# Blocks 2 and 3 of the last half of a down projection as two by two products, and the order of the last scaling

## The chip, the cores and the metric

The kernel runs on one core of one Trainium2 chip. A core has a matrix engine (TensorE, PE in the profile), a vector engine (VectorE, DVE), a scalar engine (ScalarE, ACT), GpSimd (POOL) and a queue engine (SyncE, SP); each works through its own list of instructions in order, and semaphores hold an instruction back until its inputs are there. The metric is the device time of one execution in microseconds (us); less is better. Weights stream in from HBM by DMA, matmuls read SBUF and write PSUM, which has eight banks of 512 float32 columns.

## What is computed

One layer of a streaming encoder on 512 positions of width 1024. The part that matters here is its end, the channel mixer and the final norm:

```python
    h = rms_norm(x, norm_ffn_g[l])
    up = causal_dwconv(h @ w_up[l], conv_ffn_w[l])
    a, b = jnp.split(up, 2, axis=-1)
    x = x + (jax.nn.silu(a) * b) @ w_down[l]
return rms_norm(x, norm_f_g)
```

`w_up` is 1024 x 5632, `w_down` 2816 x 1024. In front of this stand a norm, an input projection, a gated convolution and an attention branch, and their merge.

## The kernel before

All activations are kept transposed: 128 channels on the partitions and 512 positions along the free axis, as two halves of 256. Every product is made in a split precision: an operand is cut into a high part (rounded to the matmul's format, ScalarE, L245 for weights) and a low part (the rest, VectorE, L249), and a product is three matmuls of 128 x 128 by 128 x 256: high by high, low by high, high by low. The cut of a chunk of weights is called its split.

The 22 blocks of 128 hidden channels are made in two phases (`PHASES`): 12 blocks, then the part of the down projection that uses them, then 10 blocks and the rest of the down projection. The output has eight blocks `m` of 128 channels; `x1[:, m, :]` holds the running sum.

**Two by two steps.** For a pair of output blocks `i` (blocks 2i and 2i+1) and a pair of depth blocks `q` (2q and 2q+1), the four block products over both halves of the positions are made with seven products instead of eight. The seven use forms of the right operand: the blocks b11, b12, b21, b22 themselves and t1 to t4, differences of them. They lie in `gh` (high parts) and `gl` (low parts) at the pair's place with an offset: 0 is b11, 1 and 2 are b21 and b22, 3 and 4 are t1 and t2, 5 and 6 are t3 and t4, 7 is b12. `PROD` (L305) lists for each product the weight form, the offset, the bank and the half. A step takes two (i, q), and two chunks of weights: P with 6 x 128 columns (18 matmuls) and F with 8 x 128 columns (24 matmuls). F consists of sums of weight blocks that DMAs have made in DRAM long before: `group` lists three copies on SP's queue (L132) and three accumulating DMAs on POOL's queue (L135) for every two steps, and `tick` issues the next of them at certain chunks (L150). A chunk's matmuls with high weights come first, those with low weights last (`passes`, L284).

After the last step of an `i`, `combine` puts its four banks together into the two blocks: one ScalarE copy (L1029) and seven VectorE operations (L1030 to L1048). In the last phase `final_square` follows for each block: ScalarE squares it (L1060 or L1063), VectorE adds that to `ssq3` (L1064) and ScalarE multiplies the block by the norm's weights (L1065).

In the last phase, pairs i = 2 and i = 0 (blocks 4, 5, 0, 1) are done in five steps of two, numbered here 12 to 16, so P12, F12, ... F16. Blocks 2, 3, 6 and 7 are done as plain products over the last ten depth blocks (`PLAIN`), whose weights come in six chunks dp0 to dp5 cut at `PCUTS`. Blocks 2 and 3 come first, each with one matmul group, one add (L1154) and a final square. Blocks 6 and 7 come last and by halves of the positions: both blocks' first half (`pdA`), then the second half (`pdB`), and in between and behind it the sum of squares over the partitions by matmuls with ones (`pc_n`, L337), the reciprocal root (L342, L344), its spread over the partitions (`pb_n`, L351) and the scaling and the stores (`fin_out`, L1183).

**What sets the order.** TensorE's instructions run in the order written. On ScalarE and VectorE a scheduler orders the rest at build time: it follows the kernel's work in a model of its own and gives an engine, when it is free, the ready instruction that stands first in the program. Two rules are laid over that. A chunk's split goes into one of two buffers in turn, so it must wait for the matmuls of the chunk two before it: the high part for those with high weights, the low part for those with low weights. And small work (combinations, squares, the forms of a pair) is put on a list `later` with a cost in us; each split takes from the list what fits its budget (L205, budgets at L255: 1.6 us for a P chunk, 0.75 for F, 3.5 for a dp chunk), and what it takes is issued behind that split on its engine. `flush` empties the list up to what a step needs: the forms of a pair before its first use, or the readers of a bank before it is used anew.

The forms of the last pair, q = 10, are put on the list for the splits of P13 to P15: t1 and t3 at F13, t2 and t4 and the split of b11 and b12 at P14, then (L1002 for high, L1003 for low parts) b21 and b22 at F14, t3 with t4 and t1 with t2 at P15. Five buffers hold raw weights on their way from HBM (`load`, L202).

Of the kernel before, what the change touches and what calls it, by code (L numbers as in the profile page):

```python
# [10 lines left out]
AF = mybir.ActivationFunctionType  # L11
ALU = mybir.AluOpType

P = 128
# [32 lines left out]
STEPS = (  # L47
    tuple(((i, q), (i, q + 1)) for i, q in ((0, 0), (0, 2), (1, 0), (1, 2), (0, 4), (1, 4)))
    + tuple(((i, q), (i, q + 1)) for i in (3, 2) for q in (0, 2, 4)),
    (((2, 6), (2, 7)), ((2, 8), (2, 9)), ((0, 6), (0, 7)), ((0, 8), (2, 10)), ((0, 9), (0, 10))),  # L50
)
HELD = 2
GS = 3
NFF = len(STEPS[0]) + len(STEPS[1])

PLAIN = [(m, k) for m in (2, 3, 6, 7) for k in range(*PHASES[1])]
PCUTS = (0, 8, 16, 20, 28, 32, 40)


@with_exitstack  # L60
def block_kernel(ctx, tc, xT, vecs, wv, win, wmix, wo, wup, wst, wdp, outT):
# [54 lines left out]
    sums = {}  # L116
    groups = [[NFF + 2 * j, NFF + 2 * j + 1] for j in range(KB - GS)]
    ngate = len(groups)
    groups += [list(range(n, min(n + 2, NFF))) for n in range(0, NFF, 2)]
    todo = []  # L120

    def group(i):

        ns = groups[i]
        t = dsp.tile([P, len(ns), D], F32, tag=f"sum{i}", name=f"sum{i}")
        for k, n in enumerate(ns):
            sums[n] = t[:, k, :]
        w = wst[ns[0] : ns[-1] + 1].rearrange("n p c -> p n c")
        w, f = ((lambda a, b, z=z: z[:, :, a * P : b * P]) for z in (w, t))

        def copy(dst, src):
            return lambda: keep(nc.sync.dma_start(dst, src))  # L132

        def add(dst, src):
            return lambda: keep(nc.gpsimd.dma_start(dst, src, accum_op=ALU.add))  # L135

        return [
            copy(f(0, 4), w(6, 10)),
            add(f(0, 4), w(0, 4)),
            copy(f(4, 6), f(0, 2)),  # L140
            add(f(4, 6), w(2, 4)),
            copy(f(6, 8), f(4, 6)),
            add(f(6, 8), w(4, 6)),
        ]
# [7 lines left out]
            todo.pop(0)()  # L152

    def double(n):
        return [(f"P{n}", wst[n, :, : 6 * P], 6 * P), (f"F{n}", sums[n], D)]

    def gate_n(j):
        return [NFF + 2 * (j - GS) + d for d in range(2)]
# [147 lines left out]
        (1, 0, 2, 0), (2, 1, 0, 0), (6, 2, 0, 1), (0, 6, 1, 0), (3, 3, 1, 1), (5, 4, 2, 1), (4, 5, 3, 0),  # L306
    )

    def place_of(f, s_):
        c = 2 * (f % 3 if f < 6 else 3) + s_  # L310
        return slice(c * P, (c + 1) * P)

    def pair(ns, form, banks):
# [756 lines left out]

    def down(ph, n0):

        sets = ({0: X, 1: Y, 3: X, 2: Y}, {0: X, 2: Y})[ph]
        todo, wants = [], {}
        for n, d in enumerate(STEPS[ph]):
            for kind in "PF":
                prods = []
                for s_, (i, q) in enumerate(d):
                    for f, g, b, h in PROD:
                        if (f < 3) == (kind == "P"):  # L1080
                            wants.setdefault(f"{kind}{n0 + n}", []).append(("q", q))
                            prods.append((place_of(f, s_), i, place(ph, q) + g, b, h))
                todo.append((f"{kind}{n0 + n}", prods))
        users = [{(i, b) for _, i, _, b, _ in prods} for _, prods in todo]
        for n, (name, prods) in enumerate(todo):
            wh, wl = chunk(name)
            flush(wants[name])
            before = set().union(*users[:n])
            after = set().union(*users[n + 1 :])
            out = []  # L1090
            for cs, i, g, b, h in prods:
                if i not in open_:
                    flush(sets[i])
                    open_[i] = [bank(x, f"dn{ph}{i}{x}") for x in sets[i]]
                out.append((
                    open_[i][b][:, th[h]], (i, b), wh[:, cs], wl[:, cs], gh[:, g, :], gl[:, g, :],
                    (i, b) not in before and (ph, i) != (1, HELD), (i, b) not in after and (ph, i) != (0, HELD),
                ))
            passes(out, len(out))
            if name[0] == "F":  # L1100
                for i in sorted({i for _, i, *_ in prods}):
                    if (i, 0) not in after and (ph, i) != (0, HELD):
                        combine(ph, i, open_.pop(i), sets[i])
            split_next()
# [40 lines left out]
            mm3(p, wh, wl, gh[:, g, :], gl[:, g, :], opens and k == kall[0], closes and k == kall[-1])  # L1145

    plain.c = 0
    for m, b in ((2, 4), (3, 2)):
        flush((b,))
        p = bank(b, f"pd{m}")  # L1150
        for k in kall:
            for t in range(2):
                plain(m, t, (k,), p[:, th[t]], t == 0, t == 1)
        nc.vector.tensor_add(x1[:, m, :], p, x1[:, m, :])  # L1154
        later.append((0, 0.8, (), lambda m=m: final_square(m)))

    m6 = KB - 2
    fetch(3)
    wx = fp.tile([P, 6, 2 * P], F32R, tag="gr", name="wx").rearrange("p a b -> p (a b)")
    fetch(4, [wx[:, a : a + 4 * P] for a in (80, 752)])  # L1160
    fetch(5)
    flush()
    pdA, pdB6, pdB7 = bank(3, "pdA"), bank(5, "pdB6"), bank(0, "pdB7")
    pd = ((pdA[:, th[0]], pdA[:, th[1]]), (pdB6[:, th[0]], pdB7[:, th[0]]))

    def plain7(m, t, ks):
# [11 lines left out]
    def fin_col(t, sqs):  # L1178
        s_ = ssq3[:, halves[t]]
        nc.vector.tensor_add(s_, s_, sqs[0])  # L1180
        return rstd_col([s_, sqs[1]], 2, 6 + t, f"n3{t}")

    def fin_out(t, rc):  # L1183
        hs = halves[t]
        pb = rstd_bc(rc, 2, (1, 4)[t], f"n3{t}")[:, : S // 2]
        rs = fp.tile([P, S], F32, tag="fu", name=f"rs{t}", bufs=3)[:, : S // 2]
        nc.scalar.activation(rs, pb, AF.Copy)
        for g, (a, b) in enumerate(((0, 1), (1, 3), (6, 8), (3, 5), (5, 6))):
            y = x1[:, a:b, hs]
            eng, r = (nc.gpsimd, rs) if g == 2 else (nc.vector, pb)  # L1190
            eng.tensor_mul(y, y, r.unsqueeze(1).to_broadcast([P, b - a, S // 2]))
            keep((nc.sync, nc.scalar)[g % 2].dma_start(outT[:, a:b, hs], y))

    def warm_on(n):
# [1 line left out]
        for i in range(n):  # L1196
            keep(nc.tensor.matmul(warm_to, gh[:, i, :P], gl[:, i, :], start=True, stop=True))

    warm_to = bank(2, "warm_to")[:, : 2 * P]
    for m in range(2):  # L1200
        plain7(m, 0, kall)
    sqA = [fin_sum(0, 0), fin_sum(0, 1)]
# [17 lines left out]
def _layout(i):  # L1220

    import numpy as np

    i = {k: np.asarray(v) for k, v in i.items()}
    f = np.float32

    def cols(v):
        return v.reshape(-1, P).T

    def taps(w):  # L1230
        return w.reshape(3, -1, P).transpose(2, 1, 0)
# [24 lines left out]
    wvv = wi[:, 3 * CW + 2 * S : 3 * CW + 3 * S]  # L1256
    o = 3 * CW + 3 * S
    wf = wi[:, o : o + H]
    win = np.concatenate([blocks(wi[:, : 3 * CW]), blocks(wqk), blocks(wi[:, o + H :])])
    wv = np.concatenate([wvv[:, : 4 * HD], wf, wvv[:, 4 * HD :]], axis=1).reshape(KB, P, S + H)  # L1260
    wmix = np.concatenate([i["w_out_conv"][0], i["w_out_attn"][0]], axis=0)
    wup = blocks(i["w_up"][0])
    wup = np.stack([wup[:NP], wup[NP:]], axis=1).reshape(2 * NP, P, D)
    wdn = blocks(i["w_down"][0]).reshape(KB, P, NP, P)
    order = ((1, 1), (0, 0), (0, 1), (1, 0), (1, 0))
    wst = []
    for d in STEPS[0] + STEPS[1]:
        wst.append(np.concatenate([wdn[2 * i + m, :, 2 * q + k] for m, k in order for i, q in d], axis=1))
    for j in range(GS, KB):
        for d in range(2):  # L1270
            w = [
                win[20 + 8 * m + j][:, (2 * q + k) * P : (2 * q + k + 1) * P]
                for m, k in order for q in (2 * d, 2 * d + 1)
            ]
            wst.append(np.concatenate(w, axis=1))
    wst = np.stack(wst)
    wdp = np.concatenate([wdn[m, :, k] for m, k in PLAIN], axis=1)
    return {
        "xT": x.T.reshape(KB, P, S).transpose(1, 0, 2),
        "vecs": vecs,  # L1280
        "wv": wv,
        "win": win,
        "wmix": blocks(wmix),
        "wo": blocks(i["w_o"][0]),
        "wup": wup,
        "wst": wst,
        "wdp": wdp,
    }
# [24 lines left out]
```

## Time and profile before

| | us |
|---|---|
| median of 3 runs | 705.13 (704.12 to 705.4) |
| the profiled execution | 707.72 |
| its span, first to last instruction | 706.0 |
| steps of the last phase | 643.27 to 667.07 |
| blocks 2 and 3, plain | 667.07 to 680.67 |
| blocks 6 and 7, plain, first half | 680.67 to 687.47 |
| rest: second half, norm, scaling, stores | 687.47 to 706.0 |

Positions are counted from the start of the span. An entry of a timeline gives the start, the time (of a merged entry, from its first start to its last end), the engine, the line, the operation, its output and inputs, and in brackets the idle time before it and what ended it. A VectorE or ScalarE operation's time includes the end of its pipeline, so that the next can start a little before it is over. The granted clock of TensorE is 0.993 of full over the span.

### The profile page before, as it was taken

The page shows a single profiled execution, that of the slowest core. Times are in us where ns is not written, and L with a number is a line of the kernel's source. Part 1 is how long each engine was busy: PE and PEld are TensorE (multiplying, and loading weights), DVE is VectorE, ACT ScalarE, POOL GpSimd, SP SyncE. Part 2 cuts the span into 40 slices and gives each one's busy share as a digit, 9 for nine tenths or more (in the row PEclk, how much of TensorE's full clock was granted, in tenths as well). Part 3 has the DMA queues.
Part 4 walks back from the last instruction along what each step waited for, and adds up shares of the span by engine and source line. Part 5 has one row for each costly group of instructions (what it writes and reads, how often), then busy time and mean ns, then how long its engine had stood idle before and what let it go on. Part 6 is the DMA issues. An engine that isn't in the chain of part 4 may idle for free.

```text
span 706.0 us, 14566 instructions
## 1 busy us (share of the span) xinstructions
PE 694.1 (98%) x6017; PEld 692.2 (98%) x6017; DVE 494.1 (70%) x790; ACT 340.2 (48%) x538; POOL 155.8 (22%) x177
## 2 busy tenths in 40 slices
PE   9999999999989999999999999999999999999995
PEld 9999999999989999999999999999999999999995
DVE  6677777765586777764368777777774677877853
ACT  6664655544474444444354444545443344544642
POOL 4125645435221010224412122120000111100002
PEclk9999999999999999999999999999999999999998
DMA  8534776847864696866566675537765233224503
GB/s 280 167 130 99 178 205 149 197 86 214 208 179 128 180 243 212 278 208 186 103 156 166 193 144 167 143 83 231 206 201 155 90 100 111 84 83 130 177 1 120
DMA packets 49682, 112.42 MB, mean 159 GB/s; under 512 B 4656, under 2 KB 21168, under 8 KB 49616
## 3 DMA queue, kind: packets, MB, share of 16 engines
q1 hardware_dynamic: 35776, 91.89, 40.4%
q0 software_dynamic: 12576, 18.39, 16.2%
q10 hardware_dynamic: 1264, 1.22, 0.5%
q8 instruction: 47, 0.77, 0.5%
q14 instruction: 19, 0.16, 0.1%
HBM read 109.31 MB, written 30.41 MB: 198 GB/s over the span
## 4 chain that ended last, share of the span: by engine, by line
PE 92%; DMA 3%; DVE 1%; ACT 1%; issue 1%; POOL 1%; DVEq 0%; POOLq 0%; ACTq 0%
PE p_up L278 26%; PE dn L296 11%; PE p_in L278 10%; PE p_up L296 8%; PE gs L296 7%; PE p_wo L278 6%; PE yc L296 3%; PE ya L278 3%; PE p_g L278 3%; PE pd L278 2%; PE pa L457 2%; DMA sum<-in_wst_dram 2%; PE pb L459 2%; PE p_q L278 2%; PE p_k L278 2%; PE o L638 1%
## 5 line engine op out<-in xcount | busy, mean ns | idle before, releaser
L278 PE MATMUL p_up<-x1h,wh_up 128*128 128x256 f32 x536 | 104.6, 276 | 0.0
L278 PE MATMUL p_up<-x1h,wl_up 128*128 128x256 f32 x536 | 104.4, 276 | 0.0
L278 PE MATMUL p_up<-x1l,wh_up 128*128 128x256 f32 x536 | 104.3, 276 | 0.0
L245 ACT ACTIVATE wh_up<-raw_up 128x1024 fp32r<-128x1024 f32 x44 | 46.7, 1060 | 89.1 <-PE p_up L278 68.8
L278 PEld LDWEIGHTS p_up<-x1h,wh_up 128*128 128x128 f32 x536 | 80.8, 188 | 0.0
L278 PEld LDWEIGHTS p_up<-x1h,wl_up 128*128 128x128 f32 x536 | 80.7, 188 | 0.0
L278 PEld LDWEIGHTS p_up<-x1l,wh_up 128*128 128x128 f32 x536 | 80.7, 188 | 0.0
L135 POOL DMA_DIRECT2D sum<-in_wst_dram x42 | 44.9, 1080 | 108.6 <-DMA sum<-sum 79.2
L249 DVE TENSOR_TENSOR wl_up<-raw_up,wh_up 128x1024 fp32r<-128x1024 f32 x44 | 53.8, 1223 | 20.6 <-ACT wh_up L245 20.6
L278 PE MATMUL p_in<-xgh,wh_in 128*128 128x256 f32 x288 | 56.9, 279 | 1.0 <-ACT wh_in L245 1.0
L278 PE MATMUL p_in<-xgh,wl_in 128*128 128x256 f32 x288 | 56.5, 277 | 0.0
L278 PE MATMUL p_in<-xgl,wh_in 128*128 128x256 f32 x288 | 56.5, 277 | 0.0
L245 ACT ACTIVATE wh_F<-raw_F 128x1024 fp32r<-128x1024 f32 x27 | 28.7, 1064 | 51.3 <-PE ya L278 22.9
L963 DVE TENSOR_TENSOR fz<-p_up,rb_n 128x512 f32<-128x512 f32 x44 | 30.2, 689 | 31.6 <-PE p_up L278 31.6
L976 POOL TENSOR_TENSOR ge<-fu,fu 128x512 f32<-128x512 f32 x11 | 17.1, 1551 | 150.4 <-DVE fu L552 137.5
L278 PEld LDWEIGHTS p_in<-xgh,wh_in 128*128 128x128 f32 x288 | 44.7, 188 | 1.9 <-ACT wh_in L245 1.2
L249 DVE TENSOR_TENSOR wl_F<-raw_F,wh_F 128x1024 fp32r<-128x1024 f32 x27 | 33.0, 1224 | 16.6 <-ACT wh_F L245 16.6
L278 PEld LDWEIGHTS p_in<-xgl,wh_in 128*128 128x128 f32 x288 | 43.6, 188 | 0.0
L278 PEld LDWEIGHTS p_in<-xgh,wl_in 128*128 128x128 f32 x288 | 43.5, 188 | 0.0
L296 PE MATMUL p_up<-x1h,wh_up 128*128 128x256 f32 x168 | 40.3, 277 | 0.0
L296 PE MATMUL p_up<-x1l,wh_up 128*128 128x256 f32 x168 | 40.2, 276 | 0.0
L249 DVE TENSOR_TENSOR wl_in<-raw_in,wh_in 128x1024 fp32r<-128x1024 f32 x26 | 32.2, 1239 | 5.9 <-ACT wh_in L245 5.5
(307 smaller groups left out, 2045.6 us busy)
## 6 DMA issues: line engine op xcount, KB each, us to landing
raw_up<-in_wup_dram SPq DMA_DIRECT2D x44, 512.0 KB, 3.5
raw_F<-sum SPq DMA_DIRECT2D x27, 512.0 KB, 4.7
raw_in<-in_win_dram SPq DMA_DIRECT2D x26, 512.0 KB, 4.2
raw_P<-in_wst_dram SPq DMA_DIRECT2D x27, 384.0 KB, 4.6
sum<-in_wst_dram POOLq DMA_DIRECT2D x27, 256.0 KB, 5.1
sum<-in_wst_dram SPq DMA_DIRECT2D x13, 512.0 KB, 5.9
sum<-in_wst_dram POOLq DMA_DIRECT2D x13, 512.0 KB, 7.3
sum<-sum SPq DMA_DIRECT2D x26, 256.0 KB, 3.8
```

Of the source, the lines that this page charges most:

```text
L135: return lambda: keep(nc.gpsimd.dma_start(dst, src, accum_op=ALU.add))
L245: ins = nc.scalar.activation(hi, raw, AF.Copy)
L249: ins = nc.vector.tensor_sub(lo, raw, hi.bitcast(F32))
L278: keep(nc.tensor.matmul(out[:, cs], w, x[:, cs], start=start and i == 0 and c == 0, stop=stop and i == 2 and c == len(cut) - 1,))
L296: keep(nc.tensor.matmul(out, wl if x == 1 else wh, xl if x == 2 else xh, start=opens and bk not in seen, stop=closes and bk not in left,))
L457: keep(nc.tensor.matmul(pa[t][:, :VW], xt, w[:, :VW], start=start, stop=stop))
L459: keep(nc.tensor.matmul(pb[t], xt, w[:, VW:], start=start and t % 2 == 0, stop=stop and t % 2 == 1))
L638: keep(nc.tensor.matmul(o[:, os_], vv[:, kb, pr, e, :], x[:, kb, cs], start=e == 0 and kb == 0 and i == 0, stop=e == 1 and kb == nk - 1 an ...
L963: nc.vector.tensor_mul(z, p, rb2)
L976: keep(nc.gpsimd.tensor_mul(ge, a.rearrange(halves_of, h=2), b.rearrange(halves_of, h=2)))
```

## The change

The pair i = 1 (blocks 2 and 3) is taken out of the plain products and into the steps of the last phase. There are eight steps now, 12 to 19. The last has one (i, q) only, so its chunks P19 and F19 are half as wide (3 x 128 and 4 x 128 columns, 9 and 12 matmuls), and its weight layout in DRAM is filled up with zeros that aren't read. The steps of i = 2 and i = 0 are put together differently: step 14 was pairs (0, 6) and (0, 7) and is (2, 10) and (0, 6). The sums of weights grow from nine groups for the steps to eleven, the last two of one step each. `PLAIN` keeps blocks 6 and 7 with chunks dp0, dp1, dp2 of 8, 4 and 8 blocks; they are fetched together in front of the plain products, dp1 into buffers of its own (`wx`). Some banks change. In `fin_out` the copy of `pb` into `rs` on ScalarE, which GpSimd's product needs, now stands behind VectorE's first product, and the products keep the program's order.

```diff
 STEPS = (
     ...
-    (((2, 6), (2, 7)), ((2, 8), (2, 9)), ((0, 6), (0, 7)), ((0, 8), (2, 10)), ((0, 9), (0, 10))),
+    (
+        ((2, 6), (2, 7)), ((2, 8), (2, 9)), ((2, 10), (0, 6)), ((0, 7), (0, 8)), ((0, 9), (0, 10)),
+        ((1, 6), (1, 7)), ((1, 8), (1, 9)), ((1, 10),),
+    ),
 )
...
-PLAIN = [(m, k) for m in (2, 3, 6, 7) for k in range(*PHASES[1])]
-PCUTS = (0, 8, 16, 20, 28, 32, 40)
+PLAIN = [(m, k) for m in (6, 7) for k in range(*PHASES[1])]
+PCUTS = (0, 8, 12, 20)
...
-    groups += [list(range(n, min(n + 2, NFF))) for n in range(0, NFF, 2)]
+    groups += [list(range(n, min(n + 2, NFF - 1))) for n in range(0, NFF - 1, 2)] + [[NFF - 1]]
+    nstep = [len(d) for d in STEPS[0] + STEPS[1]] + [2] * (2 * (KB - GS))
...
     def double(n):
-        return [(f"P{n}", wst[n, :, : 6 * P], 6 * P), (f"F{n}", sums[n], D)]
+        h = nstep[n]
+        return [(f"P{n}", wst[n, :, : 3 * h * P], 3 * h * P), (f"F{n}", sums[n][:, : 4 * h * P], 4 * h * P)]
...
-        sets = ({0: X, 1: Y, 3: X, 2: Y}, {0: X, 2: Y})[ph]
+        sets = ({0: X, 1: Y, 3: X, 2: Y}, {0: X, 2: Y, 1: Y})[ph]
...
     plain.c = 0
-    for m, b in ((2, 4), (3, 2)):
-        flush((b,))
-        p = bank(b, f"pd{m}")
-        for k in kall:
-            for t in range(2):
-                plain(m, t, (k,), p[:, th[t]], t == 0, t == 1)
-        nc.vector.tensor_add(x1[:, m, :], p, x1[:, m, :])
-        later.append((0, 0.8, (), lambda m=m: final_square(m)))
-
     m6 = KB - 2
-    fetch(3)
+    fetch(0)
     wx = fp.tile([P, 6, 2 * P], F32R, tag="gr", name="wx").rearrange("p a b -> p (a b)")
-    fetch(4, [wx[:, a : a + 4 * P] for a in (80, 752)])
-    fetch(5)
+    fetch(1, [wx[:, a : a + 4 * P] for a in (80, 752)])
+    fetch(2)
     flush()
...
         rs = fp.tile([P, S], F32, tag="fu", name=f"rs{t}", bufs=3)[:, : S // 2]
-        nc.scalar.activation(rs, pb, AF.Copy)
         for g, (a, b) in enumerate(((0, 1), (1, 3), (6, 8), (3, 5), (5, 6))):
             y = x1[:, a:b, hs]
             eng, r = (nc.gpsimd, rs) if g == 2 else (nc.vector, pb)
-            eng.tensor_mul(y, y, r.unsqueeze(1).to_broadcast([P, b - a, S // 2]))
+            keep(eng.tensor_mul(y, y, r.unsqueeze(1).to_broadcast([P, b - a, S // 2])))
+            if g == 0:
+                keep(nc.scalar.activation(rs, pb, AF.Copy))
             keep((nc.sync, nc.scalar)[g % 2].dma_start(outT[:, a:b, hs], y))
```

More of the change, by code (lines that the diff above doesn't have):

```diff
@@ L128, in group @@
         w = wst[ns[0] : ns[-1] + 1].rearrange("n p c -> p n c")
-        w, f = ((lambda a, b, z=z: z[:, :, a * P : b * P]) for z in (w, t))
+        h = nstep[ns[0]]
+        w, f = ((lambda a, b, z=z: z[:, :, a * h * P // 2 : b * h * P // 2]) for z in (w, t))
         def copy(dst, src):
@@ L307, in block_kernel, with place_of @@
     )
-    def place_of(f, s_):
-        c = 2 * (f % 3 if f < 6 else 3) + s_
+    def place_of(f, s_, h=2):
+        c = h * (f % 3 if f < 6 else 3) + s_
         return slice(c * P, (c + 1) * P)
@@ L1081, in down @@
                             wants.setdefault(f"{kind}{n0 + n}", []).append(("q", q))
-                            prods.append((place_of(f, s_), i, place(ph, q) + g, b, h))
+                            prods.append((place_of(f, s_, len(d)), i, place(ph, q) + g, b, h))
                 todo.append((f"{kind}{n0 + n}", prods))
@@ L1147, in block_kernel @@
     plain.c = 0
-    for m, b in ((2, 4), (3, 2)):
-        flush((b,))
-        p = bank(b, f"pd{m}")
-        for k in kall:
-            for t in range(2):
-                plain(m, t, (k,), p[:, th[t]], t == 0, t == 1)
-        nc.vector.tensor_add(x1[:, m, :], p, x1[:, m, :])
-        later.append((0, 0.8, (), lambda m=m: final_square(m)))
     m6 = KB - 2
-    fetch(3)
+    fetch(0)
     wx = fp.tile([P, 6, 2 * P], F32R, tag="gr", name="wx").rearrange("p a b -> p (a b)")
-    fetch(4, [wx[:, a : a + 4 * P] for a in (80, 752)])
-    fetch(5)
+    fetch(1, [wx[:, a : a + 4 * P] for a in (80, 752)])
+    fetch(2)
     flush()
-    pdA, pdB6, pdB7 = bank(3, "pdA"), bank(5, "pdB6"), bank(0, "pdB7")
+    pdA, pdB6, pdB7 = bank(6, "pdA"), bank(7, "pdB6"), bank(0, "pdB7")
     pd = ((pdA[:, th[0]], pdA[:, th[1]]), (pdB6[:, th[0]], pdB7[:, th[0]]))
@@ L1180, in fin_col @@
         nc.vector.tensor_add(s_, s_, sqs[0])
[L1181 removed]
+        return rstd_col([s_, sqs[1]], 2, 2 + t, f"n3{t}")
     def fin_out(t, rc):
@@ L1197, in warm_on @@
             keep(nc.tensor.matmul(warm_to, gh[:, i, :P], gl[:, i, :], start=True, stop=True))
-    warm_to = bank(2, "warm_to")[:, : 2 * P]
+    warm_to = bank(5, "warm_to")[:, : 2 * P]
     for m in range(2):
@@ L1267, in _layout @@
     for d in STEPS[0] + STEPS[1]:
-        wst.append(np.concatenate([wdn[2 * i + m, :, 2 * q + k] for m, k in order for i, q in d], axis=1))
+        w = [wdn[2 * i + m, :, 2 * q + k] for m, k in order for i, q in d]
+        w += [np.zeros_like(w[0])] * (10 - len(w))
+        wst.append(np.concatenate(w, axis=1))
     for j in range(GS, KB):
```

## The prediction, made before the changed kernel ran

> **What bounds the kernel now.** I read the page first, then the chain of waits of the last 65 us, then the timelines of ScalarE and VectorE beside it. The page:
>
> ```profile
> span 706.0 us, 14566 instructions
> PE 694.1 (98%) x6017; PEld 692.2 (98%) x6017; DVE 494.1 (70%) x790; ACT 340.2 (48%) x538; POOL 155.8 (22%) x177
> PE 92%; DMA 3%; DVE 1%; ACT 1%; issue 1%; POOL 1%; DVEq 0%; POOLq 0%; ACTq 0%
> ```
>
> TensorE is the bound, and 92% of the chain lies on it. So a matmul taken away is worth its spacing, if the next matmul's operands are there. The chain in the stretch that is changed (start, length, what):
>
> ```profile
> 643.27 23.80 PE dn L296 x210
> 667.07 13.60 PE pd L278 x120
> 680.67 6.80 PE pdA L278 x60
> 687.47 1.70 PE pdB L278 x15
> 689.17 0.84 PE pc_n L337 x8
> ```
>
> The pieces join without a gap: 23.80 / 210 and 13.60 / 120 are both 113.3 ns a matmul. Everything that must be ready has been ready in time. The question is whether that stays so.
>
> **The change, term by term.** *Matmuls.* Blocks 2 and 3 cost 2 x 10 x 2 x 3 = 120 matmuls as plain products. Five pairs of depth blocks in two by two form cost 5 x 7 x 3 = 105. So 15 go: 15 x 113.3 ns = **-1.70 us**. The steps end at 643.27 + 315 x 0.1133 = 678.97 if nothing waits; call that moment T (a matmul's own row starts 0.16 earlier than in the chain: 666.91 below against 667.07).
>
> *Steady work.* Steps with a combination beside them have run before, twelve in a row:
>
> ```profile
> 477.35:534.47 57.12, 57.12 (x507) 57.12 (x506) 42.44 (x57) 27.19 (x33) 1.63 (x2) 1.00 0.71 217
> ```
>
> 57.12 us is 504 x 113.3 ns, with VectorE busy for 42.44 and ScalarE for 27.19. I cost the splits and combination of full steps at nothing; uncovered, one low part is 1.23 us. The two more groups of weight sums mean six more copies on SP's queue and six more adds on POOL's, in the ticks from step 7 to about the ninth chunk of the second half of the up projection:
>
> ```profile
> L135 POOL DMA_DIRECT2D sum<-in_wst_dram x42 | 44.9, 1080 | 108.6 <-DMA sum<-sum 79.2
> 571.62 1.58 POOL L976 TENSOR_TENSOR ge<-fu,fu 128x512 f32<-128x512 f32 x1 [9.94 <-DVE fu L552]
> 564.70 43.84 SPq L202 DMA_DIRECT2D raw_up<-in_wup_dram  x9
> ```
>
> POOL has 9.94 us free before such a product and an add takes 1.08. SP issues nine loads in 43.84 us, and five buffers hold some 20 us of weights. I take zero; a copy that keeps loads back for less than those 20 us costs nothing either.
>
> *The wait at step 14.* Pair 10 (h blocks 20 and 21) is finished last, and its first use moves from step 15 to the head of step 14. ScalarE, VectorE and TensorE there:
>
> ```profile
> 649.43 0.85 ACT L245 ACTIVATE wh_P<-raw_P 128x768 fp32r<-128x768 f32 x1 [1.20 <-PE dn L296]
> 650.18 0.61 ACT L1002 ACTIVATE gh<-ge 128x512 fp32r<-128x512 f32 x1
> 651.92 1.06 ACT L245 ACTIVATE wh_F<-raw_F 128x1024 fp32r<-128x1024 f32 x1 [1.13 <-PE dn L296]
> 650.31 0.96 DVE L249 TENSOR_TENSOR wl_P<-raw_P,wh_P 128x768 fp32r<-128x768 f32 x1
> 651.19 0.42 DVE L997 SCALAR_TENSOR_TENSOR go<-go 128x256 f32<-128x256 f32 x1
> 651.52 0.68 DVE L1003 TENSOR_TENSOR gl<-ge,gh 128x512 fp32r<-128x512 f32 x1
> 652.12 0.42 DVE L998 SCALAR_TENSOR_TENSOR go<-go 128x256 f32<-128x256 f32 x1
> 653.02 1.23 DVE L249 TENSOR_TENSOR wl_F<-raw_F,wh_F 128x1024 fp32r<-128x1024 f32 x1 [0.47 <-ACT wh_F L245]
> 653.20 0.28 PE L296 MATMUL dn<-gl,wh_P 128*128 128x256 f32 x1
> 655.94 1.29 DVE L1003 TENSOR_TENSOR gl<-go,gh 128x512 fp32r<-128x512 f32 x2
> 657.39 0.28 PE L296 MATMUL dn<-gh,wh_P 128*128 128x256 f32 x1
> ```
>
> Today the last low forms end at 655.94 + 1.29 = 657.23, 0.16 us before step 15 begins (657.39). In step 14 the sixth matmul, at 653.20, reads the low part of form 6, and form 6 is t4, the last one computed. t4 ends at 652.12 + 0.42 = 652.54. The flush for step 14 now emits the three remaining high and low pairs in front of F14's split, but each engine takes what is ready. F14's high part is ready at 651.92, before t4. ScalarE, which does t1/t2's high part (0.61) from about 651.65, therefore gives F14's 1.06 us from 652.20 and form 6's high part only from 653.17 to 653.80. VectorE, through with b21/b22's and t1/t2's low parts at 653.65, finds F14's low part ready and form 6's not: 1.23 us, pipelined into 1.15, then 0.68, to 655.48. With 0.05 us of hand-over TensorE goes on at 655.53: **+2.33 us**. If ScalarE took form 6 first, it would be 652.57 + 0.62 + 0.03 + 0.68 + 0.05 = 653.95, +0.75. With t4 straight behind t2 as well, 653.5, +0.3. One more 0.60 us product ahead makes 2.9. I take 2.33, since readiness by these rows decides; range 0.3 to 2.9.
>
> *The wait at the first plain chunk.* A chunk's high part goes into the buffer of the chunk two before it, as soon as that one's products with the high weights are through:
>
> ```profile
> 663.71 1.06 ACT L245 ACTIVATE wh_dp<-raw_dp 128x1024 fp32r<-128x1024 f32 x1 [0.94 <-PE dn L296]
> 664.80 1.23 DVE L249 TENSOR_TENSOR wl_dp<-raw_dp,wh_dp 128x1024 fp32r<-128x1024 f32 x1
> 666.91 0.28 PE L278 MATMUL pd<-gh,wh_dp 128*128 128x256 f32 x1
> ```
>
> Now 664.80 + 1.23 = 666.03 is 0.9 us early, because a full F chunk (24 matmuls, 2.72 us) runs meanwhile. Behind a half step only 12 matmuls run, 1.36 us, and three more with P19's low weights (0.34 us) after the buffer is free. So the high part starts at T - 1.66, both parts take 1.06 + 0.03 + 1.23, and the low part ends at T + 0.66. The second plain matmul is due by its row at T - 0.05 and starts at T + 0.70: **+0.75 us**. If ScalarE is still in a final scaling then, 1.08. A lower bound is 0.75, since both engines are assumed free.
>
> *The wait at the last plain chunk.* VectorE's queue behind dp0's low part: the last square of block 1, then the whole combination of blocks 2 and 3, and only then dp2's low part. Such operations, back to back:
>
> ```profile
> 663.75 0.42 DVE L1030 TENSOR_TENSOR cz<-dn,cz 128x256 f32<-128x256 f32 x1
> 664.08 0.41 DVE L1038 TENSOR_TENSOR x<-dn,x 128x256 f32<-128x256 f32 x1
> 664.41 0.41 DVE L1037 TENSOR_TENSOR cu<-dn,cz 128x256 f32<-128x256 f32 x1
> 665.95 0.68 DVE L1041 TENSOR_TENSOR x<-x,dn 128x512 f32<-128x512 f32 x1
> 666.54 0.69 DVE L1044 TENSOR_TENSOR x<-x,cz 128x512 f32<-128x512 f32 x1
> 667.15 0.69 DVE L1048 TENSOR_TENSOR x<-x,cu 128x512 f32<-128x512 f32 x1
> ```
>
> One of 256 columns starts 0.33 us after the last one, one of 512 0.60. From T + 0.57: five of 512 (3.00) and three of 256 (0.99) bring VectorE to T + 4.56, dp2's low part to T + 5.79. TensorE, going on at T + 0.70, reaches the second matmul of dp2 36 matmuls later, at T + 4.78, and starts it at T + 5.83: **+1.05 us**. This holds if the squares of blocks 2 and 3 stay behind; with one or both in front it is 1.65 or 2.25; with dp2 in front of the combination, 0. Before, two single adds stood in the place of that combination.
>
> *The last scaling.* ScalarE, VectorE, POOL:
>
> ```profile
> 699.18 0.38 ACT L1187 ACTIVATE rs<-pb_n 128x256 f32<-128x256 f32 x1 [1.95 <-PE pb_n L351]
> 699.59 1.95 DVE L1191 TENSOR_TENSOR x<-x,pb_n 128x256 f32<-128x256 f32 x4 [2.05 <-ACT rs L1187]
> 699.64 1.27 POOL L1191 TENSOR_TENSOR x<-x,rs 128x512 f32<-128x512 f32 x1 [1.32 <-ACT rs L1187]
> ```
>
> VectorE starts when ScalarE's read of the same bank ends (699.56). Turned round, the first product runs from 699.18 to 699.60, the copy to 700.02, the second product from about 700.07 instead of 699.92 (699.59 + 0.33): the later products and their stores come 0.15 late, POOL's 0.45, only the first store is earlier. **+0.15 us**. If the second product need not wait for the copy, -0.4; if POOL's store ends last, +0.45. The Trainium skill (PSUM — Partial Sum Buffer, "PSUM bank collisions raise a hardware error") says that two engines may not touch one bank at once, readers included; by that the second product waits and it is +0.15, and if readers were free it would be -0.4. The rows agree with the waiting.
>
> **Sum:** -1.70 + 2.33 + 0.75 + 1.05 + 0.15 = **+2.6 us**. The profiled execution took 707.72 us, 1.7 of it outside its span; the median of the runs is 705.13. The terms are differences, so I add them to the median: 707.7 us.
>
> **Rivals.** *Form 6 first.* ScalarE takes t4's high part ahead of F14: all the rest as above, +1.0, 706.1 us. For it: it stands first in the program. Against it: F14 is ready 0.6 us sooner. *The operands come in time (the other side).* One mechanism: VectorE's and ScalarE's order puts each operand that TensorE needs next ahead of combinations and splits. It decides at T + 4.78 for dp2 and at 653.20 for form 6. Then -1.70 + 0.3 + 0.75 + 0 - 0.4 = -1.05, 704.1 us; were form 6 and dp0 covered as well, -2.1 and 703.0, below which nothing leads. Against it: the combination stands ahead of dp2 in the program, and everything in it is ready. *Longer waits.* The highest prices together are 2.9 + 1.08 + 2.25 + 0.45 - 1.70 = +5.0, 710.1 us. The same side has a clock rival: TensorE slows after its longest wait. The first matmuls of the kernel show such a state:
>
> ```profile
> 6.67 0.43 PE pb L459 x2
> 7.46 0.23 PE pb L459 x2
> ```
>
> The same two cost 0.43 and later 0.23. At that rate the rest of step 14 and its F chunk, some 30 matmuls, would cost 3 us more, 710.7. The Trainium skill (TensorE: Matmul & The Clock Gate, "Why this matters for your kernels") puts that behind idle gaps of more than about 3 us; by that rule 2.33 us stays free of it.
>
> **How the numbers follow.** Forecast 0.47 (706.4 to 708.6), form 6 first 0.22 (705.2 to 706.9), in time 0.20 (703.0 to 705.2), longer waits or clock 0.11 (above 708.6). The range of 8 in 10 is 704.6 to 709.0; outside lie about 0.12 below and 0.07 above. A measurement of this kernel can tell about 0.2%, 1.4 us, from no change: 703.7 to 706.5. Slower: 0.45 + 0.07 + 0.11 = 0.63. Same: 0.02 + 0.15 + 0.13 = 0.30. Faster: 0.07.
>
> **What would show it.** In the chain after, 315 matmuls of steps in 35.70 us without waits would refute step 14; right is a wait of TensorE for VectorE's gl<-go about 10 us into the steps, one for wl_dp at the first plain matmuls and one some 4 us later. The plain part should keep 113.3 ns a matmul. VectorE's first product should start with ScalarE's copy behind it, the second behind that. The prediction is wrong if the scheduler orders F14's split or dp2's low part otherwise than by readiness, or if the sums' copies hold loads back.

## The result, and the profile after

| | before | after |
|---|---|---|
| median, us | 705.19 (704.12 to 705.4, 4 runs) | 711.41 (708.95 to 712.02, 4 runs) |
| the profiled execution, us | 707.72 | 710.93 |
| its span, us | 706.0 | 708.9 |
| from the first matmul of the last phase's steps to the end of the span, us | 643.11 to 706.0: 62.89 | 640.64 to 708.9: 68.26 |

The changed kernel is slower: ratio 1.0077, 95% interval 1.0058 to 1.0095. The forecast of 707.7 us had the sign and missed the size; 711.41 lies above the range of 704.6 to 709.0. Six more executions of the changed kernel (e10 below) have a median of 709.68, ratio 1.0055 (1.0037 to 1.0073). The profiled executions differ by only 3.2 us because that of before had lost time of its own earlier, at 195 to 202 us; the last row compares the stretch that the change touches, **+5.37 us**. Spans are read to 0.1 us, so a difference of two stretches is good to about 0.1 us.

The page of after, the lines that were shown of before:

```profile
span 708.9 us, 14577 instructions
PE 693.3 (98%) x6002; PEld 689.9 (97%) x6002; DVE 498.0 (70%) x798; ACT 342.2 (48%) x542; POOL 161.8 (23%) x183
PE 5%; DVE 1%; ACT 0%; issue 0%; POOL 0%; DVEq 0%; ACTq 0%
```

There are 15 matmuls less, as counted, and PE's busy time is 0.8 us less, not 1.7. The last line isn't a change from 92% to 5%: this chain could be followed back only to 653.02 us. Where it breaks off is the first place to read. Some of its pieces (start, length, what) in the changed stretch:

```profile
653.02 0.04 issue
653.07 24.62 PE dn L302 x201
679.62 1.05 ACT wh_dp L251
680.73 1.11 issue
685.93 1.15 DVE wl_dp L255
687.12 2.90 PE pdA L284 x23
```

Before, PE's pieces joined without a gap up to pc_n. Now the chain starts anew at 653, and near 680 and 686 it leaves PE for work of ScalarE and VectorE. And the 201 matmuls take 24.62 us, 1.85 more than 201 x 113.3 ns.

**Step 14.** The timelines of ScalarE, VectorE and TensorE (start, time, instruction, in brackets the idle time before it and what ended it):

```profile
649.17 0.63 ACT L1008 ACTIVATE gh<-go 128x512 fp32r<-128x512 f32 x1 [0.32 <-DVE go L1003]
649.71 1.04 ACT L251 ACTIVATE wh_F<-raw_F 128x1024 fp32r<-128x1024 f32 x1
650.66 0.61 ACT L1008 ACTIVATE gh<-go 128x512 fp32r<-128x512 f32 x1
```

```profile
651.19 1.22 DVE L255 TENSOR_TENSOR wl_F<-raw_F,wh_F 128x1024 fp32r<-128x1024 f32 x1
652.33 0.68 DVE L1009 TENSOR_TENSOR gl<-go,gh 128x512 fp32r<-128x512 f32 x1
```

```profile
653.07 0.56 PE L302 MATMUL dn<-gl,wh_P 128*128 128x256 f32 x1 [1.35 <-DVE gl L1009]
653.42 0.42 PE L302 MATMUL dn<-gh,wh_P 128*128 128x256 f32 x1
653.64 0.41 PE L302 MATMUL dn<-gl,wh_P 128*128 128x256 f32 x1
656.60 0.28 PE L302 MATMUL dn<-gl,wh_F 128*128 128x256 f32 x1
656.72 0.28 PE L302 MATMUL dn<-gh,wh_F 128*128 128x256 f32 x1
```

The order is the forecast one: F14's split goes ahead of form 6 on both engines. The sixth matmul, due at 650.73, starts at 653.07. The waits in front of it are 0.23, 0.49 and 1.63 us, **2.35 us** in all. But then the matmuls come 213 ns apart instead of 113, until 656.5. The view of windows shows why (the window and its length, then busy time of PE, PEld, DVE, ACT and POOL, the granted clock, DMA share, GB/s):

```profile
646.00:650.00 4.00, 4.00 (x38) 4.00 (x37) 4.00 (x9) 2.72 (x5) 0.00 (x0) 1.00 0.74 219
650.00:653.00 3.00, 1.44 (x8) 0.84 (x7) 3.00 (x5) 1.27 (x2) 0.00 (x0) 1.00 0.58 188
653.40:656.00 2.60, 2.60 (x14) 2.60 (x14) 0.00 (x0) 0.84 (x1) 0.00 (x0) 0.50 0.52 149
657.00:659.00 2.00, 2.00 (x19) 2.00 (x19) 0.83 (x2) 0.70 (x1) 0.00 (x0) 1.00 0.26 88
```

Straight behind the waits TensorE is granted half its clock: 0.50, until about 656.5. From 653.07 to the first matmul of P15 at 659.01 it makes 37 matmuls in 5.94 us, where 37 x 113.3 ns is 4.19: **+1.75 us**.

**The first plain chunk.** ScalarE, one entry of VectorE, and TensorE's first two plain matmuls:

```profile
675.86 0.63 ACT L251 ACTIVATE wx<-raw_dp 128x512 fp32r<-128x512 f32 x1 [2.22 <-DMA raw_dp<-in_wdp_dram]
678.32 0.64 ACT L1069 ACTIVATE sq<-x 128x512 f32<-128x512 f32 x1 [0.35 <-DVE x L1050]
678.99 0.72 ACT L1071 ACTIVATE x<-x,vec 128x512 f32<-128x512 f32 x1
679.62 1.04 ACT L251 ACTIVATE wh_dp<-raw_dp 128x1024 fp32r<-128x1024 f32 x1
```

```profile
676.53 0.69 DVE L255 TENSOR_TENSOR wx<-raw_dp,wx 128x512 fp32r<-128x512 f32 x1 [1.03 <-ACT wx L251]
```

```profile
680.72 0.38 PE L284 MATMUL pdA<-gh,wh_dp 128*128 128x256 f32 x1
681.98 0.39 PE L284 MATMUL pdA<-gh,wl_dp 128*128 128x256 f32 x1 [0.88 <-DVE wl_dp L255]
```

TensorE waits 0.29 us for dp0's high part and 1.15 for its low part, and the first matmul behind such a wait takes 0.12 longer: **1.56 us**, where 0.75 were forecast. ScalarE isn't free as assumed. The scheduler has put dp1's split (`wx`, a buffer of its own that waits for no matmul) far ahead, and ScalarE stands 2.22 us for its DMA. VectorE stands 1.03 us for the high part in its turn, in front of the end of a combination. So the square that waits for the combination (678.32) comes late on ScalarE, then a weighting, and dp0's high part only behind both, at 679.62. By the forecast's count it was due at 678.92 (T is 680.58 in this execution): 0.70 us late. Five traces have this same order, and in them TensorE's wait follows ScalarE's wait for dp1's DMA:

| us | after | e10 | e2 | e3 | e6 |
|---|---|---|---|---|---|
| ScalarE waits for dp1's DMA | 2.22 | 2.04 | 2.09 | 1.89 | 2.20 |
| TensorE waits for dp0, in all | 1.44 | 1.26 | 1.30 | 1.11 | 1.42 |

The difference is 0.78 or 0.79 us in all five.

**The last plain chunk.** VectorE does dp2's low part straight behind the combination, as forecast; TensorE waits 0.94 us, with the slow first matmul **1.06**:

```profile
685.25 0.69 DVE L1054 TENSOR_TENSOR x<-x,cu 128x512 f32<-128x512 f32 x1
685.85 1.22 DVE L255 TENSOR_TENSOR wl_dp<-raw_dp,wh_dp 128x1024 fp32r<-128x1024 f32 x1
```

**The end.** ScalarE's copy, VectorE's other products and SP's three stores:

```profile
702.11 2.76 SPq L1190 DMA_DIRECT2D out_dram<-x  x3
702.17 0.38 ACT L1189 ACTIVATE rs<-pb_n 128x256 f32<-128x256 f32 x1 [2.41 <-DVE x L1187]
702.59 1.62 DVE L1187 TENSOR_TENSOR x<-x,pb_n 128x512 f32<-128x512 f32 x3 [0.51 <-ACT rs L1189]
```

The second product does wait for the copy. From the end of pb_n (701.62) to the end of the span it is 7.28 us, against 6.92 before: **+0.36**. SP gives out its last store 3.25 us behind pb_n instead of 2.82.

The sum of what was measured (the matmuls as counted): -1.70 + 2.35 + 1.75 + 1.56 + 1.06 + 0.36 = 5.38, against 5.37 in the stretch. So close an agreement is partly chance, since the stretches are good to 0.1 us. Outside the span lie 2.0 us in this execution, 1.7 in before's; these 0.3 us appear with every kernel that has the new steps, and their cause was not found.

### The profile page after: what moved, and what is told of

Read it like the earlier page. It is cut to its first block, busy times and chain, and to the rows that moved or that the text cites. A ratio compares the mean times of both kernels' runs of the same rounds, so it can differ in the third digit from the quotient of the medians.

```text
span 708.9 us, 14577 instructions
## 1 busy us (share of the span) xinstructions
PE 693.3 (98%) x6002; PEld 689.9 (97%) x6002; DVE 498.0 (70%) x798; ACT 342.2 (48%) x542; POOL 161.8 (23%) x183
## 5 line engine op out<-in xcount | busy, mean ns | idle before, releaser
L140 POOL DMA_DIRECT2D sum<-in_wst_dram x48 | 50.6, 1074 | 152.1 <-DMA sum<-sum 119.5
L251 ACT ACTIVATE wh_F<-raw_F 128x1024 fp32r<-128x1024 f32 (+1 forms) x30 | 31.4, 1048 | 54.1 <-PE dn L302 23.9
L255 DVE TENSOR_TENSOR wl_F<-raw_F,wh_F 128x1024 fp32r<-128x1024 f32 (+1 forms) x30 | 36.2, 1206 | 18.4 <-ACT wh_F L251 18.4
L251 ACT ACTIVATE wh_P<-raw_P 128x768 fp32r<-128x768 f32 (+1 forms) x30 | 25.0, 833 | 31.5 <-PE dn L302 14.8
```

Source lines behind the costliest of these rows:

```text
L251: ins = nc.scalar.activation(hi, raw, AF.Copy)
L255: ins = nc.vector.tensor_sub(lo, raw, hi.bitcast(F32))
```

## The experiments

The diffs are against the changed kernel unless another is named; ratios are against before, with their 95% interval.

**e1: pair 10 back in its old places.**

```diff
-        ((2, 6), (2, 7)), ((2, 8), (2, 9)), ((2, 10), (0, 6)), ((0, 7), (0, 8)), ((0, 9), (0, 10)),
+        ((2, 6), (2, 7)), ((2, 8), (2, 9)), ((0, 6), (0, 7)), ((0, 8), (2, 10)), ((0, 9), (0, 10)),
```

> The changed kernel with pair 10 back in the second half of step 15 (steps 14 and 15 as before the change), all else changed. Theory: TensorE's wait at step 14 (2.34 us by the trace of after) and the half clock behind it (1.75 us) both go, so 4.1 us come back: 5.4 - 4.1 = +1.3 us against the kernel before, ratio about 1.002, and the granted clock stays 1.00 from the first step to the last scaling. Rival, the half clock has another cause than that wait (the steps themselves, the two more groups of sums): only 2.3 us come back, ratio 1.0045, and a stretch of 0.5 clock is still there. Second rival, the wait only moves to the place where block pair 1 opens the banks of block pair 2: ratio stays above 1.005, with a wait for the combination at step 17.

Measured: 708.81 us, ratio 1.0052 (1.0035 to 1.0069). No wait and no half clock in the steps; the stretch is 64.73 us, +1.84. At dp0 the wait is 0.77 us, the forecast 0.75: dp1's split waits 0.67 us for its DMA, and the square and the weighting stand behind dp0's split here. But at dp2 the wait has grown from 0.94 to 2.18. So the theory was right on the steps and missed the total (+1.3 was expected). VectorE, and TensorE's waits for it (us in all, number of waits, the longest):

```profile
680.93 0.41 DVE L1044 TENSOR_TENSOR x<-dn,x 128x256 f32<-128x256 f32 x1
682.46 1.22 DVE L255 TENSOR_TENSOR wl_dp<-raw_dp,wh_dp 128x1024 fp32r<-128x1024 f32 x1
```

```profile
PE pdA L284 <- DVE wl_dp L255: 2.6, 2, 2.0
```

VectorE works without a pause from dp0's low part (676.06) to dp2's (682.46): the earlier the steps end, the later it is against TensorE. So step 14 was one bottleneck of three, and its cure gave a part to the next.

**e2: pair 10 in step 14, but second.** The first operand of step 14 is old data; form 6 is asked for seven matmuls later.

```diff
-        ... ((2, 10), (0, 6)), ((0, 7), (0, 8)), ...
+        ... ((0, 6), (2, 10)), ((0, 7), (0, 8)), ...
```

> The changed kernel with (0, 6) and (2, 10) exchanged inside step 14, so six matmuls (0.68 us) of pair 6 stand in front of those of pair 10. The wait shrinks from 2.34 to about 1.66 us in one piece. If the clock falls by how much TensorE idles in a short time and 1.7 us is enough, the half clock stays and only 0.7 us come back: +4.7 us, ratio 1.0067. If it takes more than 2 us of idling, the half clock goes too: 5.4 - 2.4 = +3.0 us, ratio 1.0042.

Measured: 708.53 us, ratio 1.0044 (1.0029 to 1.0059); stretch 65.88, +2.99. One wait of 1.64 us, and the clock stays at 1.00, as the second of the two theories had it. (e7 below has a fall behind a wait of 1.55 us, so its limit of 2 us doesn't hold in general.)

```profile
653.15 0.39 PE L302 MATMUL dn<-gl,wh_P 128*128 128x256 f32 x1 [1.36 <-DVE gl L1009]
```

```profile
653.00:656.00 3.00, 2.85 (x24) 2.85 (x25) 1.05 (x2) 0.85 (x1) 0.00 (x0) 1.00 0.48 132
```

**e3: the changed kernel with the old last scaling.**

```diff
+        nc.scalar.activation(rs, pb, AF.Copy)
...
-            keep(eng.tensor_mul(y, y, r.unsqueeze(1).to_broadcast([P, b - a, S // 2])))
-            if g == 0:
-                keep(nc.scalar.activation(rs, pb, AF.Copy))
+            eng.tensor_mul(y, y, r.unsqueeze(1).to_broadcast([P, b - a, S // 2]))
```

> The changed kernel with the last scaling as before (ScalarE's copy first, the order of the products left to the scheduler). Read from the end of the last pb_n matmul to the end of the span: 6.91 us before the change, 7.27 us in the changed kernel. Theory: the new order costs 0.15 to 0.4 us, because the products behind the first one and their stores come later, so this run is back at 6.9. Rival: that stretch varies by as much from one execution to the next, and this run lies at 7.1 to 7.3 as well.

One execution, 707.94 us, stretch 65.89. From pb_n's end to the end it is 6.84 us against 7.28: the new order costs 0.44 here. The unexpected part stands at step 14. The waits are those of the changed kernel to the hundredth (0.23, 0.49, 1.63), and the clock does not fall:

```profile
652.44 0.39 PE L302 MATMUL dn<-gl,wh_P 128*128 128x256 f32 x1 [1.36 <-DVE gl L1009]
```

```profile
650.00:653.00 3.00, 1.36 (x7) 0.93 (x7) 2.39 (x4) 0.64 (x2) 0.00 (x0) 1.00 0.54 172
653.00:656.00 3.00, 3.00 (x29) 3.00 (x28) 0.96 (x1) 0.85 (x1) 0.00 (x0) 1.00 0.34 115
```

So the half clock is no fixed price of these waits; it follows in some executions only.

**e4: before with the new last scaling alone** (the edit of e3 the other way, in the kernel before).

> The kernel before with the new order of the last scaling alone. Theory: +0.15 to +0.4 us, which the times can hardly tell (ratio 1.000 to 1.0006); the stretch from the end of the last pb_n matmul to the end of the span is 7.1 to 7.3 us instead of 6.91, the second product starts when ScalarE's copy ends. Rival: the first store, 0.4 us earlier, lets the stores end earlier, and the stretch is 6.5 us.

Measured: 705.79 us (10 runs), ratio 1.0009 (0.9999 to 1.0018); from pb_n's end 6.94 us against 6.92. The second product starts when the copy ends here too. Taken alone the new order gains nothing and costs at most 0.2%; the 0.36 to 0.44 us that it costs behind the new steps did not show here. SP gives out its last store 3.23 us behind pb_n instead of 2.82, as in after; why the span doesn't grow by it stays open.

**e5: the half step at 18 instead of 19.**

```diff
-        ((1, 6), (1, 7)), ((1, 8), (1, 9)), ((1, 10),),
+        ((1, 6), (1, 7)), ((1, 8),), ((1, 9), (1, 10)),
```

> The changed kernel with the half step at 18 instead of 19, so that a full step stands in front of the plain products; pair 10 stays at the head of step 14. Theory: the waits at the first plain products (0.30 + 1.15 us, and 0.12 of a slow first matmul) go, because 24 matmuls now cover dp0's split; dp2's low part stays behind the combination (about 1.2 us); step 14 keeps its 2.34 us and, by chance, the half clock. +5.4 - 1.4 = +4.0 us, ratio 1.0057. Rival, dp0 waits for ScalarE and VectorE being late and not for its buffer: the wait stays within 0.3 us of what it was, ratio 1.0077.

Measured: 709.43 us, ratio 1.0052 (1.0036 to 1.0068); stretch 65.57. Step 14 waits as in after (0.24, 0.48, 1.63) with the clock at 1.00. At dp0 0.25 us are left of 1.44. A full F chunk stands in front of dp0 and covers its split; but dp1's split also waits only 0.53 us for its DMA here, so this run doesn't tell the two apart. At dp2 0.97, unchanged.

**e6: the combination of blocks 2 and 3 and their squares behind dp2's split.**

```diff
+    waiting = later[-8:]
+    del later[-8:]
     fetch(0)
...
     fetch(2)
+    later.extend(waiting)
     flush()
```

> The changed kernel with the combination and squares of blocks 2 and 3 put behind dp2's split on every engine. Theory: dp2's wait of 0.94 us (and 0.12 behind it) goes and nothing comes in its place, since VectorE has until about 8.5 us after the last step to finish: +5.4 - 1.1 = +4.3 us, ratio 1.006. Rival: the wait moves to the column sums (pc_n), which need the squares of blocks 2 and 3: a wait of 0.5 us or more in front of pc_n, ratio 1.007.

Measured: 708.5 us, ratio 1.0046 (1.0029 to 1.0063); stretch 65.57. The wait at dp2 is gone, those at step 14 and dp0 remain, the clock stays at 1.00. So what dp2's low part waited for was VectorE's combination.

**e7: all cures together, with the new last scaling**: the edits of e1, e5 and e6, and dp1's split held behind dp0's.

```diff
-    fetch(1, [wx[:, a : a + 4 * P] for a in (80, 752)])
+    with after_split():
+        fetch(1, [wx[:, a : a + 4 * P] for a in (80, 752)])
```

> All three cures together: pair 10 back in step 15, the half step at 18, the combination of blocks 2 and 3 behind dp2's split (and dp1's split behind dp0's, so that its load can't hold up the steps). If the three waits are the whole loss, the 15 matmuls saved show: -1.7, with about +0.4 for the last scaling, +0.3 outside the span as in the other runs with the new steps, and 0 to 0.7 us of wait for the squares at pc_n: -1.0 to -0.3 us against the kernel before, ratio 0.9986 to 0.9996, all matmuls from the first step to pc_n 113 ns apart, no stretch of half clock there. Rival, the two more groups of sums or the combination itself cost time elsewhere: ratio above 1.001 although these waits are gone.

**e8: the same with the old last scaling.**

> e7 with the last scaling as before. Theory: the new order costs 0.4 us at the end, so this is 0.4 us below e7, ratio 0.998 to 0.9990, and the stretch from the last pb_n matmul to the end is 6.9 us against 7.3 in e7. Rival, the order makes no difference in time: both ratios agree within 0.0003.

Measured: e7 706.86 us (12 runs), ratio 1.0016 (1.0002 to 1.0031); e8 706.86 us (12 runs), ratio 1.0012 (1.0001 to 1.0024). The three waits are gone in both, and in both a new one of 1.55 us stands in front of pc_n, longer than the 0 to 0.7 us that were allowed for; so both ratios lie above their forecasts. From pb_n's end to the end of the span it is 7.3 us in e7 and 6.9 in e8, as expected, but the medians agree, so the times don't show this difference. In e7 the half clock follows the wait (688.69 to 692.10), in e8 not:

```profile
688.02 0.58 PE L343 MATMUL pc_n<-ones,ssq 128*128 128x1 f32 x4 [1.39 <-DVE ssq L1181]
```

```profile
688.60:691.20 2.60, 2.60 (x14) 2.60 (x15) 0.16 (x1) 0.00 (x0) 0.71 (x1) 0.52 0.00 0
```

VectorE in e8, the end of its queue in front of pc_n:

```profile
683.42 0.70 DVE L1054 TENSOR_TENSOR x<-x,cu 128x512 f32<-128x512 f32 x1
684.02 0.43 DVE L1173 TENSOR_TENSOR x<-pdA,x 128x256 f32<-128x256 f32 x1
685.29 0.70 DVE L1070 TENSOR_TENSOR ssq<-ssq,sq 128x512 f32<-128x512 f32 x1
686.35 0.42 DVE L1181 TENSOR_TENSOR ssq<-ssq,sq 128x256 f32<-128x256 f32 x1 [0.36 <-ACT sq L1175]
```

It has no pause from 678.90 to 685.99, and at the end it waits for ScalarE, which weights blocks 2 and 3 ahead of the square that is asked for. e8's stretch is 62.73 us, -0.16: the 1.70 us of the matmuls less the 1.55 us of the wait.

**e9: from e8, the weighting of blocks 2 and 3 behind their squares, and pc_n two steps later.**

```diff
-        nc.scalar.activation(y, y, AF.Copy, scale=col(GF + m))
+        if ph_last[0] and m in (2, 3):
+            scales.append(lambda: nc.scalar.activation(y, y, AF.Copy, scale=col(GF + m)))
+        else:
+            nc.scalar.activation(y, y, AF.Copy, scale=col(GF + m))
...
-    plain7(0, 1, kall[:5])
+    for scale in scales:
+        scale()
+    plain7(0, 1, kall[:7])
     rcA = fin_col(0, sqA)
-    plain7(0, 1, kall[5:])
-    fin_out(0, rcA)
+    plain7(0, 1, kall[7:])
     sqB = [fin_sum(1, 0)]
-    plain7(1, 1, kall)
+    plain7(1, 1, kall[:2])
+    fin_out(0, rcA)
+    plain7(1, 1, kall[2:])
```

> All cures of e8 (pair 10 back, half step 18, combination behind dp2's split, dp1's split behind dp0's, old last scaling), and against its last wait: ScalarE's weighting of blocks 2 and 3 is put behind its squares, and the sum of the first columns is taken seven steps into dpB6's second half instead of five (0.68 us later). Theory (the change costs by waits in the stretch from the first step to the end, nothing else): e8's 1.55 us in front of the sum go, nothing waits between the steps and the sum, the stretch from the first matmul of the steps to the end is 62.89 - 1.70 = 61.2 us, and with the 0.3 us that all kernels with the new steps have outside the span the ratio is 0.998. Rival (VectorE is short of time in this stretch whatever the order, because the fifteen matmuls less leave its work where it was): a wait of 0.5 us or more stands again in front of the sum, of the spread (pb_n) or behind the second half, and the ratio is 1.000 or above.

Measured: 704.7 us (12 runs), ratio 0.9987 (0.9974 to 1.0); stretch 61.73, -1.16. In front of pc_n 0.62 us are left, so both had a share: the theory in the ratio, the rival in the wait.

**e10: the changed kernel once more.**

> The changed kernel unaltered, for how often the half clock follows its waits. Theory (the waits of 2.35 us at step 14 are in every execution, the half clock behind them, 1.75 us, in some only): the same three pieces 0.23, 0.49 and 1.63 us in the profile, with or without a clock of 0.50 behind them, and times in two groups some 1.8 to 3 us apart, about 708.5 to 709 without it and 710.5 to 712 with it. Rival (the half clock comes with the chip or the day, not with the waits): all runs in one group.

Measured: 709.68 us, six executions from 709.02 to 710.84. The profile has the same three waits (0.24, 0.49, 1.63) and the half clock behind them:

```profile
653.20:656.20 3.00, 3.00 (x17) 3.00 (x16) 0.58 (x1) 0.84 (x1) 0.00 (x0) 0.50 0.39 123
```

The two groups aren't clear cut. Of all ten executions of the changed kernel the four with a mean granted clock of 0.997 took 708.95 to 709.54 us, the six with 0.994 or 0.995 took 709.82 to 712.02. Half a clock for 3.4 us takes 1.7 off 709, 0.0024 of the mean, so this fits; but e2 has 708.62 us at 0.995 with no fall at its wait, so the mean clock alone doesn't prove a fall at step 14. The clock also falls behind the last matmuls of every profiled execution, in e2 for the last 6.4 us of the span and in after for the last 4.6, and that is in the mean too.

**e11: from e9, pc_n two steps later again.**

```diff
-    plain7(0, 1, kall[:7])
+    plain7(0, 1, kall[:9])
     rcA = fin_col(0, sqA)
-    plain7(0, 1, kall[7:])
+    plain7(0, 1, kall[9:])
     sqB = [fin_sum(1, 0)]
-    plain7(1, 1, kall[:2])
+    plain7(1, 1, kall[:4])
     fin_out(0, rcA)
-    plain7(1, 1, kall[2:])
+    plain7(1, 1, kall[4:])
```

> e9 with the sum of the first columns two steps later still (nine instead of seven, 0.68 us) and its spread four steps into dpB7's second half instead of two. Theory (e9's last wait, 0.62 us in front of the sum, is only the sum being asked for too early): the wait goes, the stretch from the first matmul of the steps to the end falls from 61.73 to about 61.1 us, the ratio is 0.998. Rival (what is put off comes back at the end: the spread's scaling then stands on VectorE in front of the last add, as VectorE has 1.95 us of it to do): the last add comes late by up to 1 us, the stretch stays at 61.7 us or grows, ratio 0.999 or above.

Measured: **703.98 us (12 runs), ratio 0.9971 (0.9959 to 0.9983)**, faster than both kernels. The stretch runs from 642.80 to 704.0: 61.2 us, -1.69. The chain of waits:

```profile
642.96 35.70 PE dn L302 x315
678.66 6.80 PE pdA L284 x60
685.46 3.06 PE pdB L284 x27
688.52 0.79 PE pc_n L343 x8
```

315 matmuls in 35.70 us, then 60 and 27, and no gap up to pc_n: the theory held, and nothing came back at the end. This is what the new steps are worth when nothing has to wait: the 15 matmuls, in full.

## Why the prediction was wrong

| term | predicted | measured in after | the runs behind it |
|---|---|---|---|
| 15 matmuls less | -1.70 | -1.70 (counted) | e11: stretch -1.69 |
| form 6 at step 14 | +2.33 | +2.35 | e1: 0; e2: 1.64 |
| the clock behind it | 0 (rival: +3) | +1.75 | e10 too; e3, e5, e6 with the same idle time: 0 |
| dp0 behind the half step | +0.75 (up to 1.08) | +1.56 | e1: 0.77; e5: 0.25 |
| dp2 behind the combination | +1.05 | +1.06 | e6: 0 |
| last scaling | +0.15 (up to 0.45) | +0.36 | e3: 0.44 less without it |
| sum | +2.6 | +5.4 | |

**Two steps failed.** The first is the last sentence of the rivals: "by that rule 2.33 us stays free of it", with 0.11 for the longer waits and the clock rival together. The Trainium skill (TensorE: Matmul & The Clock Gate, "Why this matters for your kernels") speaks of gaps above about 3 us. Here the measurement decides: 2.35 us in three pieces were enough in two profiled executions of the changed kernel. The evidence was in the trace of before, in a place that wasn't read because the change doesn't touch it. Its timeline and its windows:

```profile
196.00 0.50 PE L278 MATMUL p_g<-xgh,wh_in 128*128 128x256 f32 x2 [0.62 <-ACT wh_in L245]
197.64 0.50 PE L278 MATMUL p_g<-xgh,wl_in 128*128 128x256 f32 x2 [1.14 <-DVE wl_in L249]
```

```profile
196.00:200.00 4.00, 2.86 (x15) 2.66 (x16) 4.00 (x8) 3.69 (x6) 1.71 (x3) 0.80 0.34 84
200.00:204.00 4.00, 4.00 (x29) 4.00 (x29) 3.83 (x7) 2.07 (x3) 1.04 (x2) 0.78 1.00 272
```

Two waits of 0.62 and 1.14 us, and the clock falls (0.80 and 0.78 are means; within them it is 0.50 from 198.37 to 201.78). The forecast should have given the clock case a chance near one half, as two of five say. Its size was taken too high, +3, because the state was assumed to last for all the rest of the step; it lasts 3.41 us and costs half of that.

The second is dp0's term: "So the high part starts at T - 1.66", with 0.75 as a lower bound "since both engines are assumed free" and 1.08 as upper end. The mechanism was right and the size wrong: the high part started at T - 0.96, because the split of dp1, which has a buffer of its own (as dp4 had before) and so was not kept behind the steps, stood for its DMA and made the square and the weighting in front of dp0 late. The prediction left out that the moved fetch of dp1 also moves ScalarE's wait for its data. It also had no term for the slow first matmul behind a wait, 0.12 us each at dp0 and dp2. Without the clock, the terms as measured and the 0.3 us outside the span give 705.19 + 3.63 + 0.3 = 709.1, where the executions with the higher mean clock lie (708.95 to 709.54), at the upper end of the range and just above it. The clock alone was enough to leave the range (707.7 + 1.75 = 709.5); dp0's 0.81 us alone was not (708.5).

**Right** were the 15 matmuls, the order of F14's split and form 6 on both engines, the combination ahead of dp2, the second product behind the copy, and that the six more copies and adds of weight sums cost nothing (PE has no pause between 215 and 640 us). The sign was right for the reasons given, waits that outweigh the matmuls. The rival "the operands come in time" did not come about by itself: it took four edits by hand (e7), the old last scaling (e8) and the moves of e9 and e11 to put the operands in time.

## What to carry to other kernels

Fewer matmuls on a full TensorE are only worth their time if the other engines' work in that stretch fits into what is left; here VectorE had to end its queue 1.7 us earlier, and each cure passed the wait to the next operand until squares, weightings and the norm's sum had been put behind what TensorE asks for. Before a wait is priced by its length, search the whole trace for waits of that length and read the clock in the windows behind them. A chunk with a buffer of its own is free to be split early; if its data isn't there, it holds the engine's queue.

## What the runs showed of the hardware

The granted clock falls to 0.50 behind idle times well under 3 us, and not each time. Waits of 2.35 us in all within about 2.7 us: it fell in two of five profiled executions (after, e10; not e3, e5, e6). 1.55 us in front of pc_n: in e7, not in e8. The waits near 196 us, 1.1 to 1.8 us of idle time in all: in before and e7, in none of the other eleven. Each of these five falls lasted 3.41 us (653.13 to 656.54 in after, 653.17 to 656.59 in e10, 198.37 to 201.78 in before, 197.17 to 200.58 and 688.69 to 692.10 in e7) and cost about half of that, and it set in between 0.1 and 0.7 us after the matmuls had begun again.

Where the falls can set in can be read from the traces. Every profiled execution shows one more fall, behind its last matmuls (704.33 us in after), and in the four of them with several falls these lie whole multiples of 3.413 us apart: 15 in after (653.13 and 704.33) and in e10 (653.17 and 704.37), 147 in before (198.37 and 700.13), 144 and 4 in e7 (197.17, 688.69 and 702.34). Counted back in that step from the last fall, the three waits of step 14 lie in one window in after (649.71 to 653.13) and in e10, and TensorE was busy for 1.8 of its 3.41 us. In e2, e3 and e6 a border between two windows (652.46, 651.58 and 652.21) cuts the long wait, no window there has less than 2.3 us busy, and the clock stays. So it is in good part the position of the waits in the windows that decides. The limit isn't shown: in e5 the long wait lies in one window with 1.84 us busy, and e7 and e8 have 2.03 and 2.02 in the window of their wait for pc_n; of these three only e7 has a fall. The Trainium skill (TensorE: Matmul & The Clock Gate, "What's actually happening") describes an activity window of about 3.4 us that runs freely, not tied to the kernel's start. The lengths and the multiples agree with that; but it asks for an idle window, and here windows in which TensorE was busy for 1.65 us (before) to 2.03 us (e7) were enough.

The first matmul behind a wait took 0.11 to 0.12 us longer than the next ones (0.39 against 0.28 us in e3's and after's rows) even where the clock stayed at 1.00, at dp0 and dp2 behind waits from 0.24 us (e5) to 2.17 us (e1).
